# Three VectorE intermediates moved from SBUF to PSUM, and a later turn for the variance sum

## The chip, the cores and the metric

One Trainium2 chip, one core of it. The metric is the device time of one execution in microseconds. TensorE (PE in the rows) multiplies matrices from SBUF into PSUM; VectorE (DVE), ScalarE (ACT) and GpSimd (POOL) do elementwise work; SyncE (SP) issues the transfers. All operands of GpSimd in this kernel are in SBUF.

## The reference

Two layers over 512 latent tokens of width 2048, all in float32. Each weight is split into a rounded part and a rest (`whi`, `wlo`), so that every product is three matmuls.

```
# even layer, path A (chunked spatial gating), one of 8 channel groups g
v     = rms_norm(gelu(h @ Wav)) split into 4 chunks of 128 positions
mixed = einsum('qp,npc->nqc', w_s[g], v[:, :, g]) + b_s[g]
ya    = gelu(h @ Wau) * mixed * silu(h @ Wag)
# path B: differential attention; then x1 = x + gt * (concat(ya, yb) @ Wout)

# odd layer (Conformer convolution module)
y = a * sigmoid(b)                        # a, b, g = split(h @ w_in, 3)
y = depthwise_conv31(y) + dw_b
y = silu(layer_norm(y, ln_g, ln_b))       # mean and variance over 2048 channels
x = x1 + gt * ((y * silu(g)) @ w_out)
```

## The kernel before

Activations stand with channels on the 128 partitions and the 512 tokens along the row, so a tile is 128x512 float32 and there are 16 of them per tensor (`KT` = 16). Weights come in granules of 1 MB: SP loads `raw` (3 buffers), ScalarE rounds it to `whi` (line 100), VectorE or GpSimd takes the difference `wlo` (line 101), 2 buffers each. A granule of the odd layer feeds 48 matmuls of 512 columns (4 output tiles x 4 input tiles x 3 products).

A scheduler of the language sets the order of every engine's instructions from the order of the code and from its own guess of durations; the order is fixed when the kernel is built. Three places matter here.

1. **Mixing**, lines 637 to 656. Twice (`ug`), four groups: ScalarE makes `gu` = gelu (3 buffers), TensorE makes the mixing product `z` in a PSUM slot, VectorE computes `mx = z*gvh + bsb` (line 651) and `mx = mx*gu` (line 655), and SP stores `mx` (2 buffers) to `ug_s`. The PSUM pool `psM` has two slots of one bank; `zt()` and later `z4()` take them in turn, and the first tiles of the attention stage (`fm`, line 726) take the same two. When attention begins, SP's queue holds behind the last store of `mx` the loads of `kk` and `qq` (lines 763 and 766), whose memory overlaps what mixing used.
2. **Layer norm**, `ln_chain`, lines 1067 to 1088. It is a generator: each granule of the last gate groups (`g_group`, lines 1090 to 1092) takes one step of it through its hook. `mb` is the mean, spread by a matmul; VectorE subtracts it from the 16 tiles `zs` (line 1071), ScalarE squares (`sq`, 2 buffers), VectorE adds the squares into `vacc` (line 1077). TensorE then sums `vacc` over the partitions (line 920, in `token_rstd`), GpSimd takes the power, TensorE spreads the result (line 201), VectorE multiplies (line 1082), ScalarE applies gain and bias (1083) and tanh (`th`, 1085, 2 buffers of the same tag as `sq`), and VectorE finishes the swish (line 1086).
3. **The products for the output**, lines 1095 to 1100: `zs*sg` (line 1097), its rounding `y2h` (line 108) and rest `y2l` (line 109), read by the last 256x3 matmuls. In the same stretch GpSimd makes the `wlo` of each granule.

Of the kernel before, what the change touches and what calls it, by code (L numbers as in the profile page):

```python
# [13 lines left out]
AF = mybir.ActivationFunctionType  # L14
ALU = mybir.AluOpType
# [4 lines left out]
P = 128  # L20
D = 2048
KT = D // P
T = 512
NT = T // P
# [21 lines left out]
def hybrid_layers_kernel(  # L46
# [7 lines left out]
    V, A, G, PE, SP = nc.vector, nc.scalar, nc.gpsimd, nc.tensor, nc.sync  # L54
# [7 lines left out]
    def nm(s):  # L62
        uid[0] += 1
        return f"{s}_{uid[0]}"

    def mm(o, l, r, start, stop):
        return PE.matmul(o, l, r, start=start, stop=stop)  # L67
# [44 lines left out]
    def t_group(W, c0, mov, pool, tag, ntile=4, nk=4, lo_eng=None, hook=None, prologue=None):  # L112
        ncols = ntile * P
        ps = [pool.tile([P, T], F32, tag=tag, name=nm("tg")) for _ in range(ntile)]
        for gi in range(KT // nk):
            hi, lo = load_w(W, gi * nk * P, nk, c0, ncols, lo_eng)
            for j in range(ntile):
                for k in range(nk):
                    kt = gi * nk + k
                    mh, ml = mov[kt]  # L120
                    wh, wl = hi[:, k, j * P : (j + 1) * P], lo[:, k, j * P : (j + 1) * P]
                    mm(ps[j], wh, mh, kt == 0, False)
                    mm(ps[j], wl, mh, False, False)
                    mm(ps[j], wh, ml, False, kt == KT - 1)
            if hook:
                hook(gi)
        return ps
# [60 lines left out]
    def rstd_cols(dst, src, scale, tmp):  # L188
        n = dst.shape[1]
        V.tensor_scalar(tmp, src, scale, EPS, op0=ALU.mult, op1=ALU.add)  # L190
        G.tensor_tensor(dst, tmp, mhalf[:, 0:1].broadcast_to([P, n]), op=ALU.pow)  # L191

    def spread_cols(dst_ps, col, diag):
        n = col.shape[1]
        V.tensor_tensor(
            diag.rearrange("p (t q) -> p t q", q=P),
            ident.unsqueeze(1).broadcast_to([P, n, P]),
            col.unsqueeze(2).broadcast_to([P, n, P]),
            op=ALU.mult,
        )  # L200
        PE.matmul(dst_ps, ones, diag, start=True, stop=True)
# [9 lines left out]
    gvh = cp.tile([P, 8], F32, name="gvh")  # L211
# [15 lines left out]
    def zt(n=T):  # L227
        return psM.tile([P, n], F32, tag="m", name=nm("z"))
# [24 lines left out]
    th = tp.tile([P, 2 * KT], F32, tag="small", name="th")  # L253
# [347 lines left out]
    bsb = c2.tile([P, 8, P], F32, name="bsb")  # L601
# [35 lines left out]
    for ug in range(2):  # L637
        ps = t_group(e_w_in, C_U + 512 * ug, hm, psA, "m", hook=hook2)
        for j in range(4):
            g = 4 * ug + j  # L640
            gu = bp.tile([P, T], F32, tag="gu", bufs=3, name=nm("gu"))
            A.activation(gu, ps[j], AF.Gelu)
            z = zt()
            for n in range(NT):
                o_ = z[:, n * P : (n + 1) * P]
                vh, vl = vn[n][0][:, g * P : (g + 1) * P], vn[n][1][:, g * P : (g + 1) * P]
                mm(o_, vh, wsh[:, g, :], True, False)
                mm(o_, vh, wsl[:, g, :], False, False)
                mm(o_, vl, wsh[:, g, :], False, True)
            mx = bp.tile([P, T], F32, tag="mx", name=nm("mx"))  # L650
            V.scalar_tensor_tensor(
                mx.rearrange("p (n q) -> p n q", q=P), z.rearrange("p (n q) -> p n q", q=P), gvh[:, g : g + 1],
                bsb[:, g, :].unsqueeze(1).broadcast_to([P, NT, P]), op0=ALU.mult, op1=ALU.add,
            )
            V.tensor_tensor(mx, mx, gu, op=ALU.mult)
            SP.dma_start(ug_s[g], mx)
    p12.close()

# [248 lines left out]
    def z4(n=T):  # L907
        return psM.tile([P, n], F32, tag="m", name=nm("z4"))
# [4 lines left out]
    def tt(s, tag, bufs=1, n=T):  # L913
        return t4.tile([P, n], F32, tag=tag, bufs=bufs, name=nm(s))

    def token_rstd(acc, t0, t1, scale):
        n = (t1 - t0) // P
        z = z4(n)
        for t in range(n):
            PE.matmul(z[:, t : t + 1], acc[:, t0 + t * P : t0 + (t + 1) * P], ones[:, 0:1], start=True, stop=True)  # L920
        r = tt("r", "r", 2, n)
        rstd_cols(r, z, scale, r)
        dg = tt("dg", "b", 1, t1 - t0)
        z = z4(t1 - t0)
        spread_cols(z, r, dg)
        return z
# [83 lines left out]
    zs = [None] * KT  # L1010
# [54 lines left out]
    vacc = tt("vacc", "qacc")  # L1065

    def ln_chain():
        mb = z4()
        PE.matmul(mb, onesn, macc, start=True, stop=True)
        for i in range(KT):  # L1070
            V.tensor_tensor(zs[i], zs[i], mb, op=ALU.subtract)
            if i == 0:
                A.activation(vacc, zs[i], AF.Square)
            else:
                sq = tt("sq", "a", 2)
                A.activation(sq, zs[i], AF.Square)
                V.tensor_tensor(vacc, vacc, sq, op=ALU.add)  # L1077
            if i % 4 == 3:
                yield
        rb3 = token_rstd(vacc, 0, T, 1.0 / D)  # L1080
        for i in range(KT):
            V.tensor_tensor(zs[i], zs[i], rb3, op=ALU.mult)
            A.activation(zs[i], zs[i], AF.Identity, bias=g2[:, cLB + i : cLB + i + 1], scale=g2[:, cLG + i : cLG + i + 1])
            th = tt("th", "a", 2)
            A.activation(th, zs[i], AF.Tanh, scale=0.5)
            V.scalar_tensor_tensor(zs[i], th, 1.0, zs[i], op0=ALU.add, op1=ALU.mult)
            if i % 4 == 3:
                yield

    chain = ln_chain()  # L1090
    for gi in range(1, 4):
        g_group(gi, lambda gi: next(chain, None))
# [10 lines left out]
    for og in range(4):  # L1103
        ps = t_group(o_w_out, 512 * og, y2m, psA, "m", lo_eng=G)
        for j in range(4):
            i = 4 * og + j
# [3 lines left out]
            z = z4()  # L1110
# [47 lines left out]
```

## Time and profile before

| what | value |
|---|---|
| median of 3 runs | 1890.2 us (1884.23 to 1893.12) |
| the profiled execution's own time | 1880.81 us |
| its span (first to last instruction) | 1879.0 us |
| TensorE busy | 1818.0 us, 97% |
| VectorE / ScalarE / GpSimd busy | 1124.1 / 581.8 / 484.6 us (60 / 31 / 26%) |
| mean granted TensorE clock | 0.993 of full |

The span is cut into instructions; an engine's idle time is put down to whatever released it. The profiled execution lies 9.4 us below the median, just under the lowest of the three runs. Times in rows are microseconds from the start of the span.

### The profile page before, as it was taken

What the parts mean: (1) busy time and instruction counts of PE and PEld (TensorE: products, weight loads), DVE (VectorE), ACT (ScalarE), POOL (GpSimd) and SP (SyncE); (2) the same over time, 40 slices, a digit from 0 to 9 for tenths busy, and PEclk for the clock granted to TensorE, in tenths of its full rate; (3) what the DMA queues carried; (4) which work ended last, traced back from release to release, by engine and by line L of the source; (5) the groups of instructions that cost most, each with busy time, mean ns of one, the idle gap of its engine ahead of it and who ended that gap; (6) DMA issues with size and microseconds to landing.
All of it is one profiled execution on the core that took longest, in us unless ns stands there. A gap on an engine that the chain in (4) does not pass through costs nothing.

```text
span 1879.0 us, 21854 instructions
## 1 busy us (share of the span) xinstructions
PE 1818.0 (97%) x8744; PEld 1480.8 (79%) x8744; DVE 1124.1 (60%) x1527; ACT 581.8 (31%) x769; POOL 484.6 (26%) x191
## 2 busy tenths in 40 slices
PE   5999999999999999999999999999999999999998
PEld 2558888888788788888878779888888888778886
DVE  4348436367666536667664346169999999693000
ACT  3322212222331234444433335222222222473221
POOL 0002002011000122323212213345445445444431
PEclk9999999999999999999999999999999999999999
DMA  9996745648978577557645652322332332224441
GB/s 319 339 332 210 224 139 180 201 155 283 314 255 296 190 191 198 150 149 194 215 166 202 216 194 84 107 95 90 102 100 90 98 104 90 90 74 136 138 134 57
DMA packets 220390, 324.16 MB, mean 173 GB/s; under 512 B 10169, under 2 KB 139522, under 8 KB 212098
## 3 DMA queue, kind: packets, MB, share of 16 engines
q1 hardware_dynamic: 220290, 322.77, 53.9%
q8 instruction: 69, 1.13, 0.2%
q14 instruction: 31, 0.25, 0.0%
HBM read 289.18 MB, written 33.55 MB: 172 GB/s over the span
## 4 chain that ended last, share of the span: by engine, by line
PE 78%; DMA 9%; DVE 5%; issue 4%; POOL 1%; ACT 1%; SPq 1%; DVEq 0%; POOLq 0%; ACTq 0%
PE tg L67 37%; PE mb L67 17%; PE fm L67 9%; PE m L67 7%; DMA raw<-in_o_ada_w_dram 5%; PE S L67 2%; DMA raw<-in_e_ada_w_dram 2%; PE oT L67 2%; PE z L301 1%; DVE acc L460 1%; DVE wlo L101 1%; POOL wlo L101 1%; DVE vacc L1077 1%; PE t L815 1%; DMA x<-in_x_dram 1%
## 5 line engine op out<-in xcount | busy, mean ns | idle before, releaser
L101 POOL TENSOR_TENSOR wlo<-raw,whi 128x2048 fp32r<-128x2048 f32 x84 | 396.7, 4723 | 719.4 <-ACT whi L100 711.4
L100 ACT CAST whi<-raw 128x2048 fp32r<-128x2048 f32 x136 | 259.7, 1909 | 629.5 <-PE tg L67 272.6
L1041 DVE SCALAR_TENSOR_TENSOR z<-y,dwc,z 128x512 f32<-128x512 f32 x480 | 319.1, 740 | 0.1
L67 PE MATMUL tg<-h2h,wlo 128*128 128x512 f32 x704 | 275.4, 391 | 0.0
L67 PE MATMUL tg<-h2l,whi 128*128 128x512 f32 x704 | 274.6, 390 | 0.0
L67 PE MATMUL tg<-h2h,whi 128*128 128x512 f32 x704 | 271.0, 390 | 0.0
L460 DVE SCALAR_TENSOR_TENSOR acc<-raw,silu_c,acc 128x2048 f32<-128x2048 f32 x60 | 143.7, 2394 | 130.6 <-DMA raw<-in_o_ada_w_dram 82.7
L67 PE MATMUL mb<-whi,hhi 128*128 128x512 f32 x512 | 202.2, 397 | 2.6 <-ACT avt L622 2.0
L101 DVE TENSOR_TENSOR wlo<-raw,whi 128x2048 fp32r<-128x2048 f32 x52 | 119.1, 2290 | 140.1 <-ACT whi L100 140.1
L67 PE MATMUL mb<-wlo,hhi 128*128 128x512 f32 x512 | 201.2, 393 | 0.6 <-DVE wlo L101 0.6
L67 PE MATMUL mb<-whi,hlo 128*128 128x512 f32 x512 | 201.1, 393 | 0.0
L67 PEld LDWEIGHTS tg<-h2l,whi 128*128 128x128 f32 x704 | 132.6, 188 | 28.2 <-issue 0.5
L67 PEld LDWEIGHTS tg<-h2h,wlo 128*128 128x128 f32 x704 | 132.4, 188 | 27.9 <-issue 0.5
L67 PEld LDWEIGHTS tg<-h2h,whi 128*128 128x128 f32 x704 | 132.6, 188 | 27.5
L191 POOL TENSOR_TENSOR rs<-ms,mhalf 128x8 f32<-128x8 f32 x20 | 37.0, 1864 | 376.6 <-DVE ms L190 376.6
L67 PEld LDWEIGHTS mb<-whi,hhi 128*128 128x128 f32 x512 | 96.7, 189 | 36.0 <-issue 13.6
L67 PEld LDWEIGHTS mb<-wlo,hhi 128*128 128x128 f32 x512 | 96.7, 189 | 20.4 <-DVE wlo L101 1.0
L67 PEld LDWEIGHTS mb<-whi,hlo 128*128 128x128 f32 x512 | 96.7, 189 | 20.1
L67 PE MATMUL fm<-hhi,whi 128*128 128x512 f32 x256 | 106.8, 417 | 0.0
L1109 DVE SCALAR_TENSOR_TENSOR xr<-tg,gt,xr 128x512 f32<-128x512 f32 x16 | 11.9, 750 | 157.2 <-PE tg L67 125.2
L67 PE MATMUL tg<-y2h,wlo 128*128 128x512 f32 x256 | 99.9, 390 | 3.1 <-POOL wlo L101 3.1
L67 PE MATMUL fm<-hlo,whi 128*128 128x512 f32 x256 | 101.4, 396 | 0.0
(251 smaller groups left out, 3125.6 us busy)
## 6 DMA issues: line engine op xcount, KB each, us to landing
raw<-in_e_w_in_dram SPq DMA_DIRECT2D x56, 1024.0 KB, 5.3
raw<-in_o_ada_w_dram SPq DMA_DIRECT2D x48, 1024.0 KB, 6.5
raw<-in_o_w_in_dram SPq DMA_DIRECT2D x48, 1024.0 KB, 5.1
raw<-in_e_ada_w_dram SPq DMA_DIRECT2D x64, 512.0 KB, 8.2
raw<-in_e_ada_w_dram SPq DMA_DIRECT2D x16, 1024.0 KB, 5.1
raw<-in_e_w_out_dram SPq DMA_DIRECT2D x16, 1024.0 KB, 5.5
raw<-in_o_w_out_dram SPq DMA_DIRECT2D x16, 1024.0 KB, 5.1
qq<-q_s SPq DMA_DIRECT2D x16, 512.0 KB, 7.1
```

The lines of the kernel that those rows point to most:

```text
L67: return PE.matmul(o, l, r, start=start, stop=stop)
L100: A.copy(hi, raw)
L101: (lo_eng or V).tensor_tensor(lo, raw, hi.bitcast(F32), op=ALU.subtract)
L191: G.tensor_tensor(dst, tmp, mhalf[:, 0:1].broadcast_to([P, n]), op=ALU.pow)
L301: PE.matmul(ada_ps[j][32 * g : 32 * g + 32, 0 : 2 * nc_], S[:, kt, :], raw[:, i, :], start=(kt < 4), stop=(kt >= KT - 4), skip_group_check ...
L460: V.scalar_tensor_tensor(ada_state["acc"], raw, sc_[:, jt : jt + 1], ada_state["acc"], op0=ALU.mult, op1=ALU.add)
L815: PE.transpose(z[:, k * P : (k + 1) * P], e[:, (k0 + k) * P : (k0 + k + 1) * P], ident)
L1041: V.scalar_tensor_tensor(zi if t == TAPS - 1 else z, y2[:, t : t + T], w(t), z, op0=ALU.mult, op1=ALU.add)
L1077: V.tensor_tensor(vacc, vacc, sq, op=ALU.add)
L1109: V.scalar_tensor_tensor(xr, ps[j], gt2[:, i : i + 1], xr, op0=ALU.mult, op1=ALU.add)
```

## The change

Four edits. In mixing, line 651 writes its result back into the PSUM tile `z` instead of the SBUF tile `mx`, and line 655 reads `z` and `gu`; `mx` is written once. In layer norm, the running sum of squares lives in a PSUM tile `vp` taken from the pool `psM`; only the last addition writes `vacc` in SBUF, which the matmul of line 920 reads. A further `yield` stands between the last addition and `token_rstd`. And `th` is a PSUM tile from `psM` instead of an SBUF tile.

```
             z3 = z.rearrange("p (n q) -> p n q", q=P)
+            V.scalar_tensor_tensor(
+                z3, z3, gvh[:, g : g + 1], bsb[:, g, :].unsqueeze(1).broadcast_to([P, NT, P]), op0=ALU.mult, op1=ALU.add,
+            )
             mx = bp.tile([P, T], F32, tag="mx", name=nm("mx"))
-            V.scalar_tensor_tensor(
-                mx.rearrange("p (n q) -> p n q", q=P), z.rearrange("p (n q) -> p n q", q=P), gvh[:, g : g + 1],
-                bsb[:, g, :].unsqueeze(1).broadcast_to([P, NT, P]), op0=ALU.mult, op1=ALU.add,
-            )
-            V.tensor_tensor(mx, mx, gu, op=ALU.mult)
+            V.tensor_tensor(mx, z, gu, op=ALU.mult)
...
+        vp = z4()
         for i in range(KT):
             V.tensor_tensor(zs[i], zs[i], mb, op=ALU.subtract)
             if i == 0:
-                A.activation(vacc, zs[i], AF.Square)
+                A.activation(vp, zs[i], AF.Square)
             else:
                 sq = tt("sq", "a", 2)
                 A.activation(sq, zs[i], AF.Square)
-                V.tensor_tensor(vacc, vacc, sq, op=ALU.add)
+                V.tensor_tensor(vacc if i == KT - 1 else vp, vp, sq, op=ALU.add)
             if i % 4 == 3:
                 yield
+        yield
         rb3 = token_rstd(vacc, 0, T, 1.0 / D)
...
-            th = tt("th", "a", 2)
+            th = z4()
```

The built order of instructions shows what becomes of it. First VectorE in the first round of mixing (`z` and `mx` carry running numbers; `wlo` is the difference of a weight granule, `acc` a running product for the modulation vectors).

```order
-L651 SCALAR_TENSOR_TENSOR mx_4226<-z_4213,gvh,bsb 128x512
+L651 SCALAR_TENSOR_TENSOR z_4213<-z_4213,gvh,bsb 128x512
 L460 SCALAR_TENSOR_TENSOR acc_3836<-raw_4389,silu_c,acc_3836 128x2048
-L655 TENSOR_TENSOR mx_4207<-mx_4207,gu_4192 128x512
-L655 TENSOR_TENSOR mx_4226<-mx_4226,gu_4211 128x512
-L651 SCALAR_TENSOR_TENSOR mx_4245<-z_4232,gvh,bsb 128x512
-L651 SCALAR_TENSOR_TENSOR mx_4264<-z_4251,gvh,bsb 128x512
-L655 TENSOR_TENSOR mx_4245<-mx_4245,gu_4230 128x512
-L655 TENSOR_TENSOR mx_4264<-mx_4264,gu_4249 128x512
+L655 TENSOR_TENSOR mx_4208<-z_4194,gu_4192 128x512
+L655 TENSOR_TENSOR mx_4227<-z_4213,gu_4211 128x512
+L651 SCALAR_TENSOR_TENSOR z_4232<-z_4232,gvh,bsb 128x512
```

`z` is now read until line 655, so its slot comes free later; TensorE's products for `z_4232` and `z_4251` were moved behind 26 more matmuls of the weights. In the second round (`z_4527` to `z_4584`) the order is the same as before: 651 and 655 in turn.

Second, TensorE around the variance sum, line 920, before and then of the change (`tg` is an output tile of the gate product, `h2h` and `h2l` its inputs).

```order
L67 MATMUL tg_11916<-h2h_8675,wlo_12154 128x512
L67 MATMUL tg_11916<-h2l_8676,whi_12153 128x512
L920 MATMUL z_1776_11971<-ones,vacc_11616 128x1 x4
L67 MATMUL tg_11916<-h2h_8681,whi_12153 128x512
L67 MATMUL tg_11916<-h2h_8681,wlo_12154 128x512
```

```order
L67 MATMUL tg_11917<-h2h_8675,wlo_12135 128x512
L67 MATMUL tg_11917<-h2l_8676,whi_12134 128x512
L920 MATMUL z_1780_12026<-ones,vacc_11616 128x1 x4
L67 MATMUL tg_11917<-h2h_8681,whi_12134 128x512
L67 MATMUL tg_11917<-h2h_8681,wlo_12135 128x512
```

Only the numbers differ: the variance sum stands three matmuls before the end of the same granule, and the spreading matmul of line 201 stands 24 matmuls behind that granule in both. The further `yield` changes the numbering and not this place.

Third, ScalarE at the start of the tanh of layer norm, before and then of the change.

```order
L1083 ACTIVATE z_9906<-z_9906,g_86 128x512
L1083 ACTIVATE z_9940<-z_9940,g_86 128x512
L1085 ACTIVATE th_11985<-z_9906 128x512
L1083 ACTIVATE z_9974<-z_9974,g_86 128x512
L1085 ACTIVATE th_11990<-z_9940 128x512
L1083 ACTIVATE z_10008<-z_10008,g_86 128x512
```

```order
L1085 ACTIVATE z_9906<-z_9906,g_86 128x512
L1085 ACTIVATE z_9940<-z_9940,g_86 128x512
L1087 ACTIVATE z_1784_12040<-z_9906 128x512
L1085 ACTIVATE z_9974<-z_9974,g_86 128x512
L1085 ACTIVATE z_10008<-z_10008,g_86 128x512
L1085 ACTIVATE z_10510<-z_10510,g_86 128x512
```

The second tanh (`z_1785`) now stands behind 15 of the 16 gain-and-bias steps, because its PSUM slot holds the spread factor until VectorE's last multiplication; the first keeps its place. Smaller moves: the `wlo` of the first granule of the odd layer stands two additions earlier on VectorE, and TensorE's last matmuls of that part alternate between two output tiles; two loads of `xr` for the end stand some twenty loads earlier on SP.

## Rows read from the trace of the kernel before

**Rows 1.** The page, busy time by engine (busy us, share of span, instructions).

```profile
PE 1818.0 (97%) x8744; PEld 1480.8 (79%) x8744; DVE 1124.1 (60%) x1527; ACT 581.8 (31%) x769; POOL 484.6 (26%) x191
```

**Rows 2.** Waits of TensorE: who waited for whom, total us, times, longest us.

```profile
PE z L67 <- DVE mx L651: 3.8, 1, 3.8
...
PE z L920 <- DVE vacc L1077: 2.8, 1, 2.8
```

**Rows 3.** Timeline of VectorE, second mixing round: start us, us, instruction, idle before.

```profile
646.48 0.75 DVE L651 SCALAR_TENSOR_TENSOR mx<-z,gvh,bsb 128x512 f32<-128x512 f32 x1 [8.08 <-PE z L67]
647.33 4.90 DVE L655 TENSOR_TENSOR mx<-mx,gu 128x512 f32<-128x512 f32 x1
652.16 0.74 DVE L651 SCALAR_TENSOR_TENSOR mx<-z,gvh,bsb 128x512 f32<-128x512 f32 x1
...
654.74 0.75 DVE L651 SCALAR_TENSOR_TENSOR mx<-z,gvh,bsb 128x512 f32<-128x512 f32 x1 [1.04 <-DMA ug_s<-mx]
```

**Rows 4.** Timeline of GpSimd, the same stretch.

```profile
647.17 4.52 POOL L101 TENSOR_TENSOR wlo<-raw,whi 128x2048 fp32r<-128x2048 f32 x1 [1.54 <-ACT whi L100]
```

**Rows 5.** Timeline of TensorE: fourth mixing product, first attention fill.

```profile
652.95 0.45 PE L67 MATMUL z<-wsh,vnh 128*128 128x128 f32 x1 [3.83 <-DVE mx L651]
...
655.64 0.77 PE L67 MATMUL fm<-hhi,whi 128*128 128x512 f32 x1
```

**Rows 6.** Windows: us, busy us by engine (instructions), PEclk (share of full), DMA share, GB/s.

```profile
652.90:659.60 6.70, 6.65 (x21) 5.75 (x22) 3.49 (x5) 0.00 (x0) 0.00 (x0) 0.51 0.56 170
...
1638.30:1644.00 5.70, 5.70 (x22) 4.73 (x23) 2.48 (x5) 2.38 (x2) 2.03 (x2) 0.70 0.31 121
```

**Rows 7.** Timeline of SP's transfers from 645; last row: size, median us to landing.

```profile
645.66 0.37 SPq L92 DMA_DIRECT2D raw<-in_e_w_in_dram  x1
...
652.26 4.37 SPq L656 DMA_DIRECT2D ug_s<-mx  x3
656.73 0.38 SPq L92 DMA_DIRECT2D raw<-in_e_w_in_dram  x1
657.77 0.32 SPq L656 DMA_DIRECT2D ug_s<-mx  x1
663.06 1.33 SPq L763 DMA_DIRECT2D kk<-k_s  x2
...
raw<-in_e_w_in_dram SPq DMA_DIRECT2D x2, 1024.0 KB, 5.3
```

**Rows 8.** Timeline of VectorE in layer norm.

```profile
1606.84 9.65 DVE L1071 TENSOR_TENSOR z<-z,z 128x512 f32<-128x512 f32 x16 [8.36 <-PE z L1069]
1616.41 13.66 DVE L1077 TENSOR_TENSOR vacc<-vacc,sq 128x512 f32<-128x512 f32 x12
1631.51 5.47 DVE L1077 TENSOR_TENSOR vacc<-vacc,sq 128x512 f32<-128x512 f32 x2 [1.44 <-ACT sq L1076]
...
1637.49 0.68 DVE L1077 TENSOR_TENSOR vacc<-vacc,sq 128x512 f32<-128x512 f32 x1
```

**Rows 9.** Timeline of GpSimd in layer norm.

```profile
1604.61 4.61 POOL L101 TENSOR_TENSOR wlo<-raw,whi 128x2048 fp32r<-128x2048 f32 x1 [3.20 <-ACT whi L100]
1616.40 5.16 POOL L101 TENSOR_TENSOR wlo<-raw,whi 128x2048 fp32r<-128x2048 f32 x1 [7.18 <-ACT whi L100]
```

**Rows 10.** Lines 1071, 1077, 1041: durations min/median/max ns, first and last start.

```profile
L1071 DVE TENSOR_TENSOR z<-z,z x16: 677/679/689, 1606.8 to 1615.8; 128x512 f32<-128x512 f32 x16
...
L1077 DVE TENSOR_TENSOR vacc<-vacc,sq x15: 681/692/4908, 1616.4 to 1637.5; 128x512 f32<-128x512 f32 x15
...
L1041 DVE SCALAR_TENSOR_TENSOR z<-y,dwc,z x480: 728/740/756, 1240.8 to 1597.7; 128x512 f32<-128x512 f32 x160
```

**Rows 11.** Timelines of GpSimd, VectorE and TensorE where the output product begins.

```profile
1679.37 9.10 POOL L101 TENSOR_TENSOR wlo<-raw,whi 128x2048 fp32r<-128x2048 f32 x1 [7.92 <-ACT whi L100]
...
1684.57 4.45 DVE L1097 TENSOR_TENSOR z<-z,sg 128x512 f32<-128x512 f32 x1
...
1688.52 0.50 PE L67 MATMUL tg<-y2h,wlo 128*128 128x512 f32 x1 [2.15 <-POOL wlo L101]
...
1701.34 0.50 PE L67 MATMUL tg<-y2h,wlo 128*128 128x512 f32 x1 [0.95 <-POOL wlo L101]
```

More of the change, by code (lines that the diff above doesn't have):

```diff
@@ L649, in hybrid_layers_kernel @@
                 mm(o_, vl, wsh[:, g, :], False, True)
+            z3 = z.rearrange("p (n q) -> p n q", q=P)
+            V.scalar_tensor_tensor(
+                z3, z3, gvh[:, g : g + 1], bsb[:, g, :].unsqueeze(1).broadcast_to([P, NT, P]), op0=ALU.mult, op1=ALU.add,
+            )
             mx = bp.tile([P, T], F32, tag="mx", name=nm("mx"))
-            V.scalar_tensor_tensor(
-                mx.rearrange("p (n q) -> p n q", q=P), z.rearrange("p (n q) -> p n q", q=P), gvh[:, g : g + 1],
-                bsb[:, g, :].unsqueeze(1).broadcast_to([P, NT, P]), op0=ALU.mult, op1=ALU.add,
-            )
-            V.tensor_tensor(mx, mx, gu, op=ALU.mult)
+            V.tensor_tensor(mx, z, gu, op=ALU.mult)
             SP.dma_start(ug_s[g], mx)
```

## The prediction

> **What bounds the kernel.** I read the page first: TensorE is busy 97% of the span [rows 1], so only what shortens TensorE's idle time, or its stretches at half clock, can shorten the kernel. The list of TensorE's waits comes next, because it says which idle time the change can touch. Two of its entries end at instructions that the diff edits: 3.8 us in mixing and 2.8 us at the variance sum [rows 2]. Then I went to the timelines of those places. In mixing, line 655 multiplies two SBUF tiles and takes 4.90 us, not the 0.69 us of its neighbours; it begins just after GpSimd's `wlo` and ends just after it [rows 3, 4]. In layer norm the additions of line 1077 read two SBUF tiles and reach 4908 ns where the median is 692, while the subtractions of line 1071, which read one SBUF tile and one PSUM tile, stay at 677 to 689 ns although GpSimd worked beside them from 1604.61 to 1609.2 [rows 8, 9, 10]. So the reader should see one mechanism: a VectorE instruction with two SBUF inputs stands still while GpSimd's tensor operation runs, and one with a single SBUF input does not. Last, the windows: after both waits TensorE runs at half clock for a while, 0.51 granted over 6.7 us after the first, and 0.70 over 5.7 us after the second [rows 6]. A wait costs more than its length.
>
> **Mixing, second round.** What it loses now: until 655.64, when the first attention fill starts, and then at half clock until 659.6. Those 4.0 us at half clock are worth 2.0 us, so the stage ends as if it had gone on at full clock from 657.6 [rows 5, 6].
> After the change the first 651 still runs at 646.48 and 655 at 647.33, now 0.69 us long: done at 648.0 rather than 652.2. The PSUM slot is now held until 655 ends, not until 651 ends at 647.2, so the third product starts about 0.5 us late. The twelve matmuls of a product took 2.7 us at half clock [rows 5], so 1.35 at full: third product until 649.4, and the fourth, whose slot is free at 649.5 after the second 655, until 650.9. What is late next is the third 655: it writes an `mx` buffer whose store must have landed. That store is issued at 648.05, behind a 1 MB weight load issued at 645.66, which takes 5.3 us and lands at 651.0 [rows 7]. A store with nothing ahead let VectorE go on 2.5 us after its issue (652.26 to 654.74) [rows 3, 7]; behind the load I bound its end from 651.0 (rides along) to 653.5 (starts when the load has landed), and take 652.2, as the store's own 256 KB are a quarter of the load. The third 655 then runs to 652.9 and the first fill, which takes that slot, starts at 653.0 at full clock. Gain: 657.6 - 653.0 = 4.6 us, with the bounds 3.3 and 5.8.
> One limit behind it: the loads of `kk` wait for the last store, which stands behind another 1 MB load (5.3 us from 657.77 to 663.06) [rows 7]. They move with the third 655: that load issues at 653.0 instead of 656.73, so `kk` starts about 3.4 us earlier, at 659.7. The first scores come 72 matmuls after the first fill, so the loads' lead shrinks by about 1.2 us; I count nothing for it and leave it to the range, whose mixing term I cut to 5 us at the top.
>
> **Mixing, first round.** GpSimd is idle there, nothing was blocked, nothing is gained. The slot is held until 655, but the scheduler placed the third and fourth product behind 26 more matmuls (some 6 us), which covers the roughly 3 us that it takes longer. Cost nothing; without that cover it would be those 3 us.
>
> **Layer norm.** Two of the fifteen additions stood behind GpSimd: the first twelve took 13.66 us where eleven steps of 0.8 and one of 0.7 make 9.5, so 4.1 too long; the next two 5.47 for 1.5, so 4.0 too long [rows 8]. As `vp` is in PSUM, both fall away: the last addition ends near 1638.2 - 8.1 = 1630.1. TensorE reached line 920 2.8 us before 1638.2, at 1635.4 [rows 2, 8], and its place in the order has not moved. The wait goes with 5 us to spare. Price: 2.8 us, and the half clock behind it. At a granted 0.70 over 5.7 us, 3.4 us were at half, worth 1.7. With 0.2 us for starting up again, 4.7 us.
> The trace has no addition that writes PSUM. Below it lies 0.68 us (line 1071, PSUM read), above it 0.74 (line 1041, PSUM read and written) [rows 10]; at 0.74 the fifteen cost 0.9 us more, inside the 5 us. One square and sixteen tanh of ScalarE now write PSUM too. For these I take no change, as VectorE's rows show none; the square, the first of the chain, could cost its whole length again and stay inside the 5 us, and tanh runs ahead of a VectorE that is the slower there.
> [...]
> The `yield` costs nothing: TensorE's order is unchanged. `th` in PSUM: line 1086 is no longer blocked, but what follows it on VectorE, lines 1097 and 109, still reads two SBUF tiles and takes the block instead (4.45 us on line 1097 already now [rows 11]). Gain on the chain: near nothing. TensorE waits there only for `wlo`, 2.15 and 0.95 us [rows 11], since GpSimd stands still in turn while VectorE's two-input instructions follow one another (9.10 us instead of 4.6). With single-input instructions among them GpSimd gets in sooner, but TensorE also arrives sooner by the gap that goes; I take 0, with bounds -2 and +3.4.
>
> **Elsewhere.** Around 1170 the `wlo` that moved up on VectorE holds the last additions of the norm before it by 2 us; alternating matmuls cover most of it. I take -0.4 us, bounds -1.5 and +0.5.
>
> **Sum.** 4.6 + 4.7 + 0 - 0.4 = 8.9 us. The profiled execution's own time, 1880.8, becomes 1871.9. It lies 9.4 us under the median, so against the median: 1890.2 - 8.9 = 1881.3 us, -0.47%.
>
> **Rivals.**
> *A, the output product's waits go too.* For it: GpSimd's 9.10 us is caused by VectorE's two-input instructions, of which 16 go. Against: TensorE comes earlier. Then 4.6 + 4.7 + 3.1, with its two restarts, some 12.5 us: 1877.7.
> *B, the mixing gain is taken by a new wait.* The slot is held longer and the third 655 hangs on a store; if the 0.5 and 2 us that TensorE waits then bring the half clock back for as long as now (6.7 us, worth 3.4), mixing gives 1.2 us and the whole 5.5: 1884.7. For: 2.8 us idle brought it. Against: 2.15 us did not, at 1688 [rows 11].
> *C, slower: the output product becomes paced by GpSimd.* All four granules of the first output group wait for a whole `wlo` (4.6 us) and each wait brings the half clock (1.7 us): 25 us lost, 16 net, 1906. It decides from the point at which each of the four waits passes 2.2 us (8.9 in all). For: two of the four wait already, and tanh now waits for a PSUM slot. Against: fewer instructions compete with GpSimd.
>
> **Chances.** Forecast (7 to 10.5 us) 0.47; A (10.5 to 14) 0.23; B (3 to 7) 0.21; C and less than 3 us 0.09. What this kernel's measurement can tell from no change is about 0.5%, 9.5 us. Faster by more: all of A and a third of the forecast, 0.39. Slower by more: most of C, 0.05. Within: 0.56. The range, from 1875 (A at its far end, with 1 us) to 1888 (B's far end, 3 us gained, and 1 us), leaves out C and the tails of A and B. The forecast alone: 1879.7 to 1883.2.
>
> **What would show it.** Right: line 655 at 0.7 us throughout, no wait of TensorE at line 920 and none of 3.8 us in mixing, no half clock after 1638, additions of line 1078 all near 0.7 us. Wrong: a wait of the first `fm` or third `z` beyond 2.5 us; half clock at 655; waits for `wlo` near 1690 above 2.2 us each; scores waiting for `kk` or `qq`.

## The result, and the profile after

| kernel, timing | median us (runs) | kernel before beside it | ratio, 95% interval |
|---|---|---|---|
| the change, first | 1877.55 (6) | 1890.93 | 0.994 (0.9921 to 0.996) |
| the change, second | 1877.01 (6) | 1887.06 | 0.9937 (0.9913 to 0.9961) |
| the change, third | 1877.14 (11) | 1887.22 | 0.9949 (0.9931 to 0.9968) |

The change is faster by 0.5 to 0.6%, 10 to 13 us between the medians. The forecast was 1881.3, in a range of 1875 to 1888; the measured time lies in the range, and below the 1879.7 to 1883.2 of the forecast alone. The profiled execution has a span of 1876.6, only 2.4 us below that of before; why that is less than the medians say comes at the end of this section and with the first experiment.

The page of the changed kernel, busy time by engine, answers to [rows 1]. TensorE's total is the same within 0.4 us: no work has gone.

```profile
PE 1818.4 (97%) x8744; PEld 1481.2 (79%) x8744; DVE 1110.6 (59%) x1527; ACT 581.6 (31%) x769; POOL 479.6 (26%) x191
```

TensorE's waits of the changed kernel that answer to [rows 2] and [rows 11] (who waited for whom, total us, times, longest):

```profile
PE tg L67 <- POOL wlo L101: 1.9, 1, 1.9
...
PE S L67 <- ACT th L736: 1.6, 1, 1.6
PE fm L67 <- DVE mx L655: 1.4, 1, 1.4
...
PE z L67 <- DVE mx L655: 0.4, 1, 0.4
```

The 3.8 us at the fourth product (the start that [rows 5] show) and the 2.8 us at line 920 are gone. In place of the first stand 0.4 us at the third product and 1.4 at the first attention fill, and the wait at the first scores (`S`) has grown from 0.5 to 1.6.

**Mixing, second round.** VectorE, GpSimd and TensorE there, and the window behind the first fill; they answer to [rows 3 to 6].

```profile
649.16 0.76 DVE L651 SCALAR_TENSOR_TENSOR z<-z,gvh,bsb 128x512 f32<-128x512 f32 x1 [8.35 <-PE z L67]
650.01 0.69 DVE L655 TENSOR_TENSOR mx<-z,gu 128x512 f32<-128x512 f32 x1
...
651.46 0.69 DVE L655 TENSOR_TENSOR mx<-z,gu 128x512 f32<-128x512 f32 x1
...
654.41 0.69 DVE L655 TENSOR_TENSOR mx<-z,gu 128x512 f32<-128x512 f32 x1 [1.24 <-DMA ug_s<-mx]
```

```profile
649.85 4.55 POOL L101 TENSOR_TENSOR wlo<-raw,whi 128x2048 fp32r<-128x2048 f32 x1 [1.37 <-ACT whi L100]
```

```profile
655.25 0.47 PE L67 MATMUL fm<-hhi,whi 128*128 128x512 f32 x1 [1.43 <-DVE mx L655]
```

```profile
655.20:661.90 6.70, 6.65 (x29) 5.54 (x30) 1.26 (x2) 0.00 (x0) 0.00 (x0) 1.00 0.76 238
```

GpSimd's operation runs from 649.85 to 654.40, and line 655 passes it twice in 0.69 us. The third 655 waits for the store, the first fill starts 6.1 us after the first 651 (655.25 - 649.16), and the clock stays at full. Before it took 9.2 us, and then 4.0 us at half clock, worth 2.0.

The gain reaches the scores only as far as their loads come forward. TensorE's first score before, then of the change SP's last store, the first `kk` load behind it, and the first score:

```profile
674.73 0.59 PE L67 MATMUL S<-kk,qq 128*128 128x256 f32 x2 [0.51 <-issue]
```

```profile
656.58 0.32 SPq L656 DMA_DIRECT2D ug_s<-mx  x1
661.87 1.33 SPq L763 DMA_DIRECT2D kk<-k_s  x2
...
673.42 1.65 PE L67 MATMUL S<-kk,qq 128*128 128x256 f32 x8 [1.56 <-ACT th L736]
```

Counted from the first 651, the first `kk` load is issued at 16.6 us before and at 12.7 in the change, 3.9 earlier; the first score comes 11.7 us after it before and 11.6 in the change, and 11.4 to 11.7 in all six profiles with the whole mixing edit (18.9 to 19.1 after the start of the third 655). The row of the wait names ScalarE's `th`, but that had ended 0.9 us before the score, and in the run with the product in PSUM (below) it ends 0.7 us after it. So the loads, and not `th`, are what the scores hang on.

**Layer norm.** The fifteen additions, line 1078 (1077 before), and GpSimd beside them; they answer to [rows 8 to 10].

```profile
1618.37 9.54 DVE L1078 TENSOR_TENSOR z<-z,sq 128x512 f32<-128x512 f32 x12
1629.72 1.50 DVE L1078 TENSOR_TENSOR z<-z,sq 128x512 f32<-128x512 f32 x2 [1.81 <-ACT sq L1077]
...
1631.73 0.68 DVE L1078 TENSOR_TENSOR vacc<-z,sq 128x512 f32<-128x512 f32 x1
```

```profile
1618.37 4.63 POOL L101 TENSOR_TENSOR wlo<-raw,whi 128x2048 fp32r<-128x2048 f32 x1 [7.18 <-ACT whi L100]
1629.24 4.62 POOL L101 TENSOR_TENSOR wlo<-raw,whi 128x2048 fp32r<-128x2048 f32 x1 [6.24 <-ACT whi L100]
```

Twelve take 9.54 us instead of 13.66, two take 1.50 instead of 5.47, with GpSimd at work beside both. The last ends at 1632.4, and TensorE comes to line 920 at 1637.2, 4.8 us later.

**Where a loss came in**, at the norm ahead of the odd layer: TensorE's spreading matmul of line 201 and ScalarE's copy of it, first of the kernel before and then of the changed one.

```profile
1162.66 0.60 PE L201 MATMUL z<-dg,ones 128*128 128x256 f32 x2
...
1163.30 0.37 ACT L965 COPY rbs<-z 128x256 f32<-128x256 f32 x1 [1.37 <-PE z L201]
```

```profile
1164.21 0.60 PE L201 MATMUL z<-dg,ones 128*128 128x256 f32 x2
...
1164.85 0.37 ACT L965 COPY rbs<-z 128x256 f32<-128x256 f32 x1 [2.97 <-PE z L201]
...
1177.92 0.50 PE L67 MATMUL m<-h2h,wlo 128*128 128x512 f32 x1 [1.22 <-DVE wlo L101]
```

The diff does not touch these lines. The order of TensorE does change here: the spreading matmul stands 19 places later, the multiplications behind it start 1.55 us later, and TensorE ends by waiting 1.22 us for VectorE's `wlo`. How much that costs hangs on the granted clock ahead of the spreading matmul. The whole stretch (the fifth column of the table below) in the first and the second profile of the change:

```profile
1145.67:1203.97 58.30, 54.20 (x330) 48.71 (x330) 32.83 (x58) 27.51 (x46) 19.01 (x26) 0.97 0.30 95
```

```profile
1142.70:1199.99 57.29, 53.19 (x330) 47.45 (x330) 32.83 (x58) 27.51 (x46) 19.01 (x26) 1.00 0.30 97
```

At full clock the new order costs 1.0 us; with a stretch at half clock in it (0.97) 2.0, and at 0.94, in the run with the product in PSUM, 3.1. In the old order the stretch is 56.3 us at 0.97 as well as at 1.00, and 56.9 at 0.94.

**Account by stretch.** Each kernel that ran left a profile. The table has for each the time from the start of one instruction to the start of another: where the first line 651 of the second round starts (ahead of every place where I expect a gain or loss); from there to the first score; from there to GpSimd's first multiplication of the norm ahead of the odd layer (line 972); from there to GpSimd's second `wlo` after it; from the first subtraction of the layer norm to the spreading of its variance; from there to the end of the span. Before: 646.48, 674.73, 1145.72, 1202.01, 1606.84, 1647.23.

| profile | first 651 at | mixing to scores | scores to 972 | norm ahead of odd layer | variance sum | to the end |
|---|---|---|---|---|---|---|
| before | 646.48 | 28.25 | 470.99 | 56.29 | 40.39 | 231.77 |
| before, against itself | 647.56 | 28.01 | 478.59 | 56.26 | 40.37 | 232.29 |
| the change, first | 649.16 | 24.26 | 472.25 | 58.30 | 35.71 | 232.09 |
| the change, second | 647.44 | 23.43 | 471.83 | 57.29 | 35.71 | 231.77 |
| the change, third | 644.89 | 23.97 | 472.15 | 58.30 | 35.71 | 232.16 |
| only mixing | 645.81 | 23.56 | 472.86 | 58.31 | 41.65 | 231.68 |
| only variance sum | 647.78 | 28.18 | 470.45 | 56.30 | 35.71 | 232.55 |
| only tanh | 648.00 | 28.12 | 470.65 | 56.29 | 40.38 | 231.63 |
| without tanh | 647.20 | 24.24 | 472.02 | 58.33 | 35.71 | 232.58 |
| two groups | 651.72 | 25.14 | 470.77 | 56.29 | 35.71 | 231.84 |
| two groups, three mx | 651.54 | 23.89 | 481.11 | 56.88 | 35.71 | 231.85 |
| rest on VectorE | 650.89 | 28.45 | 470.00 | 56.28 | 40.34 | 232.22 |
| squares in PSUM | 644.95 | 28.06 | 472.28 | 56.28 | 35.71 | 232.60 |
| product in PSUM | 652.02 | 24.05 | 470.19 | 59.42 | 35.70 | 228.19 |

The change, as the mean of its three profiles against the first of before: -4.4 in mixing to the scores (28.25 - 23.89), +1.7 at the norm, -4.7 at the variance sum, +0.2 to the end, together -7.2 us. Two stretches are left out. From GpSimd's second `wlo` to the first subtraction it is 404.8 us in all fourteen. From the scores to line 972 the change has 1.1 us more on average; apart from the two profiles with 478.6 and 481.1, of which the first experiment speaks, that stretch goes from 470.0 to 472.9 in kernels with and without the edit, so I count it to neither. A difference of two spans says little: the first line 651 alone starts anywhere from 644.9 to 652.0, with most of that spread ahead of any edit, as the two rows of the kernel before and the three of the change show. From the first 651 to the end, the three profiles of the change are 5.1 to 7.7 us shorter than the first profile of before, and 12.9 to 15.5 shorter than the second.

### The profile page after: what moved, and what is told of

Read it like the earlier page. It is cut to its first block, busy times and chain, and to the rows that moved or that the text cites. A ratio compares the mean times of both kernels' runs of the same rounds, so it can differ in the third digit from the quotient of the medians.

```text
span 1876.6 us, 21858 instructions
## 1 busy us (share of the span) xinstructions
PE 1818.4 (97%) x8744; PEld 1481.2 (79%) x8744; DVE 1110.6 (59%) x1527; ACT 581.6 (31%) x769; POOL 479.6 (26%) x191
## 4 chain that ended last, share of the span: by engine, by line
PE 79%; DMA 8%; DVE 5%; issue 4%; POOL 1%; ACT 1%; SPq 1%; DVEq 0%; POOLq 0%; ACTq 0%
PE tg L67 39%; PE mb L67 17%; PE fm L67 9%; PE m L67 6%; DMA raw<-in_o_ada_w_dram 5%; PE S L67 2%; DVE acc L460 2%; PE z L301 2%; PE oT L67 2%; DVE wlo L101 1%; DMA raw<-in_e_ada_w_dram 1%; PE t L815 1%; POOL wlo L101 1%; DMA x<-in_x_dram 1%; DMA q_s<-qklo 0%
## 5 line engine op out<-in xcount | busy, mean ns | idle before, releaser
L101 POOL TENSOR_TENSOR wlo<-raw,whi 128x2048 fp32r<-128x2048 f32 x84 | 390.3, 4646 | 714.8 <-ACT whi L100 706.8
```

What stands on the lines that cost most here:

```text
L101: (lo_eng or V).tensor_tensor(lo, raw, hi.bitcast(F32), op=ALU.subtract)
```

## The experiments

The theories: **S**, the edits work each at its own place, with the sizes of the table; **R**, the medians moved more than these places show because the timed runs of the kernel before contain something that its first profile lacks. Other rivals are named where they are tried. In edits a line with - is of the kernel named ahead of it.

### The kernel before against itself

> The unchanged kernel against itself, to see how large a difference is without any edit and to get a second profile of it. Ratio 1.000, with an interval of about 0.3% to either side. Theory S (the gain comes from the two places alone, some 5 us in the two profiled executions once a clock drop near 515 us is left out): the second profile looks like the first, with TensorE waiting 3.8 us in mixing and 2.8 us at the variance sum, and a span within 3 us of 1879. Rival R (the timed runs of the kernel before contain something that its first profiled execution, 9.4 us below the median, did not): this profile has a span of 1885 us or more, and stretches at half clock or waits that the first one lacks.

Measured: ratio 1.0016 (1.0001 to 1.0031), 1889.25 against 1886.52. So 0.2% is what the same kernel can differ from itself, and the interval, which leaves out 1, is too narrow. The profile has a span of 1887.9, 9 us over the first one, as R said. VectorE, GpSimd and TensorE at the place that differs most, in the first profile of before, then in this one, and the window behind it:

```profile
1096.26 2.29 DVE L101 TENSOR_TENSOR wlo<-raw,whi 128x2048 fp32r<-128x2048 f32 x1
...
1096.71 6.30 POOL L101 TENSOR_TENSOR wlo<-raw,whi 128x2048 fp32r<-128x2048 f32 x1 [19.50 <-ACT whi L100]
...
1098.60 0.50 PE L67 MATMUL m<-yh,wlo 128*128 128x512 f32 x1 [2.84 <-DVE wlo L101]
```

```profile
1098.23 6.58 DVE L101 TENSOR_TENSOR wlo<-raw,whi 128x2048 fp32r<-128x2048 f32 x1
...
1098.16 4.50 POOL L101 TENSOR_TENSOR wlo<-raw,whi 128x2048 fp32r<-128x2048 f32 x1 [19.49 <-ACT whi L100]
...
1104.87 0.79 PE L67 MATMUL m<-yh,wlo 128*128 128x512 f32 x1 [7.65 <-DVE wlo L101]
```

```profile
1098.00:1110.00 12.00, 5.13 (x13) 4.08 (x14) 9.51 (x6) 2.32 (x5) 4.50 (x1) 0.57 0.60 182
```

It is the mechanism of the change at a place where the change does nothing. Two operations with two SBUF inputs each, one of VectorE and one of GpSimd, become ready together; the one that starts first takes its normal time (VectorE 2.29 us, GpSimd 4.50) and the other stands (GpSimd 6.30 us, VectorE 6.58). VectorE was 0.45 us ahead in the first profile; here GpSimd was ahead by 0.07, TensorE waited 4.8 us longer and went on at half clock, a granted 0.57 over the 12 us of the last row, and the stretch from the scores to line 972 is 7.6 us longer (table). Of the fourteen profiles GpSimd was first in two.

### The parts

Each has one part of the diff alone: the hunk of lines 650 to 655; the hunks with `vp` and `yield`; the hunk with `th`.

> Only the mixing edit. Theory S: the first attention fill starts about 6 us after the first line 651 at full clock, where it took 9.2 us and then 4 us at half clock before: -5.0 us there. Around 1160 to 1180 TensorE's order is that of the whole change (the spreading matmul 19 places later), which costs 2.6 us; the scores wait 1 us longer. Net about -1.5 us, ratio 0.999. Rival R: as the medians moved by 13 us with the whole change, this edit alone gives 6 us or more, ratio 0.997 or less.

Measured: ratio 0.9979 (0.9963 to 0.9995). The gain to the scores (23.56 us) and the loss at the norm (58.31) both belong to this edit; the wait at line 920 stays. S holds in the profile in kind (net -2.7 us for the two, where S had -1.5); the ratio lies between the two theories and its interval holds both. The stretch of the variance sum is 1.3 us longer here than before (41.65 against 40.39), behind the same wait of 2.8 us: the granted clock over the 6.7 us after it is 0.54, where before it was 0.75.

> Only the variance sum in PSUM and its later turn. No other instruction of TensorE moves. Theory S: no wait at line 920, no half clock behind it, -4.7 us, ratio 0.9975; the waits for the weight rests at the output product stay about 3 us together. Rival A: with TensorE earlier by 4.7 us the waits at the output product grow by as much, ratio 1.000. Rival R: 8 us or more, ratio 0.996 or less.

Measured: ratio 0.9975 (0.9962 to 0.9988), as S said: 35.71 us in its stretch, 56.30 at the norm. Rival A's giving back is small, 0.8 us to the end: TensorE waits 2.1 us for GpSimd at the output product, and the granted clock is 0.83 over the 10 us from 1680, where before it stayed at full.

> Only tanh in PSUM. Theory S: ratio 1.000; line 1086 stays at 0.7 us beside GpSimd where it reached 4.8, but lines 1097 and 109 take the block, and the wait at line 920 is unchanged at 2.8 us; the waits for the weight rests at the output product stay between 1 and 5 us together. Rival A: GpSimd gets in sooner, the two waits for it (2.15 and 0.95 us) go, -3 us, ratio 0.998. Rival C: tanh waiting for its PSUM slot holds up VectorE and TensorE waits 5 us or more there, ratio 1.003.

Measured: ratio 1.0015 (1.0001 to 1.003), which is what the kernel before has against itself. Two groups by line and GpSimd's timeline at the start of the output product:

```profile
L1086 DVE SCALAR_TENSOR_TENSOR z<-z,z x16: 674/678/691, 1658.9 to 1701.3; 128x512 f32<-128x512 f32 x16
...
L1097 DVE TENSOR_TENSOR z<-z,sg x16: 675/679/4614, 1659.6 to 1704.3; 128x512 f32<-128x512 f32 x16
```

```profile
1680.52 4.94 POOL L101 TENSOR_TENSOR wlo<-raw,whi 128x2048 fp32r<-128x2048 f32 x1 [7.89 <-ACT whi L100]
```

Line 1086 is never held any more, line 1097 takes the block, and GpSimd's operation shrinks from 9.10 us [rows 11] to 4.94. TensorE still waits 2.6 us there in two parts, and the stretch to the end is the same. S; the variance sum is as late as before in this kernel.

The further `yield` had no run of its own: with it alone the built order of the instructions is that of before on all five engines.

### The whole once more, and without tanh

> The whole change once more, beside its parts. Theory S (the edits add up, each at its own place): from the profiles of the parts -2.7 us for mixing (-5.65 at the place, +1.0 at the scores, +2.0 around 1170), -4.7 for the variance sum, 0 for tanh, together -7.4 us, ratio 0.996. Rival D: the edits give more together than apart, ratio 0.994 as in the first timing.

Measured: ratio 0.9937 (0.9913 to 0.9961), and 0.9949 (0.9931 to 0.9968) in a third timing.

> The whole change a third time, for comparison within this call: ratio 0.994 to 0.996.

> The whole change without the tanh edit. Theory S: tanh gives nothing, so this is as good as the whole change, ratio 0.994 to 0.996, and the waits for GpSimd at the output product are 2 to 3 us in both. Rival D (the whole is more than its parts because tanh helps once the variance sum is early): 2 us or more slower than the whole change in the same call.

Measured for the change without tanh: ratio 0.9963 (0.9946 to 0.9979), a median of 1878.58 against 1877.14 for the whole beside it. The parts give 0.9979 x 0.9975 = 0.9954 without tanh, and 0.9969 with tanh's 1.0015; the whole gives 0.9937 to 0.9949, each with some 0.2% to either side and a kernel that differs from itself by as much. S and D can't be told apart by these times. The profiles speak for D in kind and against its size: where the variance sum is early, the stretch to the end is 232.6 us in the three profiles with tanh in SBUF and 231.8 to 232.2 in the five with tanh in PSUM (the product still in SBUF), some 0.6 us less.

### The blocker is GpSimd, and two SBUF inputs

Of the kernel before:

```
-            return load_w(jobs[n][2], gi * 8 * P, 8, jobs[n][3], 2 * P, G)
+            return load_w(jobs[n][2], gi * 8 * P, 8, jobs[n][3], 2 * P, V if n == 0 else G)
```

> The kernel before, but the rests (wlo) of the first two weight granules of the attention stage are computed by VectorE, so that GpSimd stands idle beside the second round of mixing; line 655 still reads two SBUF tiles. Theory S (GpSimd's tensor operation is what holds line 655): all eight of line 655 at 0.7 us, TensorE's 3.8 us wait at the third product gone or under 1 us, no half clock behind it; less the 2.3 us each that VectorE now spends on the two rests, -3 to -5 us, ratio 0.998. Rival G (line 655 is slow for another reason, its SBUF output or the store that runs beside it): the first 655 of the second round stays near 4.9 us, ratio 1.000.

Measured: ratio 1.0013 (0.9993 to 1.0033). Line 655 by its durations (min/median/max ns), and VectorE's timeline:

```profile
L655 DVE TENSOR_TENSOR mx<-mx,gu x8: 680/682/692, 609.8 to 662.4; 128x512 f32<-128x512 f32 x8
```

```profile
650.89 0.75 DVE L651 SCALAR_TENSOR_TENSOR mx<-z,gvh,bsb 128x512 f32<-128x512 f32 x1 [2.97 <-PE z L67]
651.56 2.28 DVE L101 TENSOR_TENSOR wlo<-raw,whi 128x2048 fp32r<-128x2048 f32 x1
...
660.49 1.42 DVE L651 SCALAR_TENSOR_TENSOR mx<-z,gvh,bsb 128x512 f32<-128x512 f32 x2 [4.66 <-DMA ug_s<-mx]
```

G falls: two SBUF inputs with no GpSimd beside them run in 0.68 us. The gain that I expected did not come. VectorE's own 2.28 us stands between lines 651 and 655, a weight load slips ahead of the first store, and the third 651 waits 4.66 us for that store. TensorE waits 1.6 + 3.4 us where it waited 3.8.

Again of the kernel before:

```
-                sq = tt("sq", "a", 2)
+                sq = z4()
```

> The kernel before with one edit: the squares (sq) are PSUM tiles, while the running sum vacc stays in SBUF, read and written there. Theory S (VectorE is held only if both inputs are in SBUF): additions of 0.7 us beside GpSimd, no wait at line 920, ratio 0.9975 as with the sum in PSUM. Rival W (what counts is that the running sum is not written to SBUF): additions of 4.9 us as before, a wait of 2.8 us at line 920, ratio 1.000.

Measured: ratio 0.9972 (0.9954 to 0.999). Line 1077 of this kernel, and GpSimd beside it:

```profile
L1077 DVE TENSOR_TENSOR vacc<-vacc,z x15: 676/689/690, 1616.0 to 1629.3; 128x512 f32<-128x512 f32 x15
```

```profile
1615.96 4.63 POOL L101 TENSOR_TENSOR wlo<-raw,whi 128x2048 fp32r<-128x2048 f32 x1 [7.18 <-ACT whi L100]
```

The sum is read from and written to SBUF as before, only the second input is in PSUM, and no addition is held: the longest takes 690 ns, where the held ones of before reached 4.9. W falls: here the second SBUF input is what counts. Line 655 shows the same beside GpSimd, 4.90 us with two SBUF inputs and 0.69 with one, and at 1098 a head start of 0.07 us decided who stands, 6.58 against 2.29 us for VectorE.

### Taking the loss back

Of the changed kernel; the second of the two runs has the last line as well (and so has the other tile of that tag, `junk`). Lines below stand one further in these kernels: 652 and 656.

```
+            mx = bp.tile([P, T], F32, tag="mx", name=nm("mx"))
+            m1 = z if ug and j < 2 else mx
             V.scalar_tensor_tensor(
-                z3, z3, gvh[:, g : g + 1], bsb[:, g, :].unsqueeze(1).broadcast_to([P, NT, P]), op0=ALU.mult, op1=ALU.add,
+                m1.rearrange("p (n q) -> p n q", q=P), z.rearrange("p (n q) -> p n q", q=P), gvh[:, g : g + 1],
+                bsb[:, g, :].unsqueeze(1).broadcast_to([P, NT, P]), op0=ALU.mult, op1=ALU.add,
             )
-            V.tensor_tensor(mx, z, gu, op=ALU.mult)
+            V.tensor_tensor(mx, m1, gu, op=ALU.mult)
...
+            mx = bp.tile([P, T], F32, tag="mx", bufs=3, name=nm("mx"))
```

> The whole change, but in mixing only the first two groups of the second round keep their result in PSUM, the six others go through mx as before. TensorE's spreading matmul then stands one place later around 1160, not nineteen. Theory S (the one thing that mixing gains is the first line 655 of the second round, and what it loses around 1170 is the later spreading matmul): first attention fill as early as with the whole edit, no second wait there, 2.0 to 2.6 us better than the whole change, ratio 0.995. Rival E: the loss around 1170 is not from that order, ratio as the whole change.

> As the run with two groups, and mx has three buffers, so that the third group does not wait for the landing of the first store. Theory S: the wait of the first attention fill (1.4 us) goes, and 1.0 to 1.4 us are gained on top of the run with two groups, ratio 0.9945. Rival F: the scores wait for their loads behind the same 1 MB weight loads as before, so that what is gained at the fill is lost at the scores, ratio as the run with two groups.

Measured: ratios 0.9958 (0.9939 to 0.9977) and 0.9968 (0.9948 to 0.9988). With two groups the stretch of the norm is 56.29 us again, so the loss comes from the order there, as S said. VectorE's `wlo` is back in its old place too; that the spreading matmul is what counts is read from the rows above, where the multiplications are late ahead of any `wlo`. But the mixing stretch is 25.14 us, where the whole edit has 23.4 to 24.3, because the third line 652 writes `mx` again and waits 2.53 us for the store. S had the fill as early as with the whole edit; it comes 6.4 us after the first 652. TensorE at the first fill, and the window behind it:

```profile
658.14 0.47 PE L67 MATMUL fm<-hhi,whi 128*128 128x512 f32 x1 [1.75 <-DVE mx L652]
```

```profile
658.10:664.10 6.00, 5.96 (x19) 4.82 (x20) 2.04 (x3) 0.00 (x0) 0.00 (x0) 0.72 0.67 203
```

The wait is 1.75 us, and half clock is back. With three buffers the first fill waits for nothing and comes 4.5 us after the first line 652, and then the scores stand, with the clock down behind them:

```profile
675.43 2.85 PE L67 MATMUL S<-kk,qq 128*128 128x256 f32 x8 [2.85 <-issue]
```

```profile
672.00:684.00 12.00, 9.15 (x36) 7.30 (x35) 3.22 (x6) 3.75 (x6) 1.79 (x1) 0.86 1.09 232
```

Rival F: what is won at the fill is lost at the scores. This profile is also the second in which GpSimd was first at 1099 (8.7 us of wait there), and both kernels are no better than the change.

### One operation more

Of the changed kernel:

```
+        yp = z4()
-        V.tensor_tensor(zs[i], zs[i], sgs[i], op=ALU.mult)
+        V.tensor_tensor(yp, zs[i], sgs[i], op=ALU.mult)
         hi, lo = htile("y2h"), htile("y2l")
-        split(hi, lo, zs[i])
+        split(hi, lo, yp)
```

> The whole change, and the product of line 1099 goes into a PSUM tile, from which ScalarE rounds it and VectorE takes the rest: 16 more VectorE instructions read one SBUF input, the 16 of line 1099 still read two. Rival A of the prediction (the waits for GpSimd at the output product can go as well): GpSimd gets in between, its first wlo there takes under 6.5 us where it took 9.1, the waits of TensorE for it (1.9 to 2.7 us) go, 2 to 4 us better than the whole change, ratio 0.992. Theory S: the block moves to the 16 that are left and the two PSUM slots hold VectorE up instead; the waits stay or grow, ratio 0.994 to 0.997.

Measured: ratio 0.9931 (0.9911 to 0.9952), a median of 1873.65 (6 runs) where the change beside it had 1877.14. The same window of TensorE in the kernel before, the change and this one:

```profile
1676.00:1716.00 40.00, 36.90 (x162) 29.90 (x161) 28.93 (x36) 19.45 (x26) 22.25 (x4) 1.00 0.28 92
```

```profile
1676.00:1716.00 40.00, 38.12 (x161) 31.07 (x160) 26.49 (x32) 17.45 (x24) 18.70 (x4) 0.96 0.24 79
```

```profile
1676.00:1716.00 40.00, 40.00 (x178) 33.13 (x177) 29.98 (x34) 16.68 (x24) 18.88 (x4) 1.00 0.24 81
```

No wait and no half clock is left in it, and the stretch to the end is 228.2 us where it was 231.8 and 232.1. The waits that rival A named are gone, worth 3.9 us against the change, from an edit that this change doesn't have. Its mechanism is not shown: GpSimd's operation there, in the change and then in this kernel, is no shorter.

```profile
1692.48 4.56 POOL L101 TENSOR_TENSOR wlo<-raw,whi 128x2048 fp32r<-128x2048 f32 x1 [10.79 <-ACT whi L100]
```

```profile
1688.83 5.05 POOL L101 TENSOR_TENSOR wlo<-raw,whi 128x2048 fp32r<-128x2048 f32 x1 [7.88 <-ACT whi L100]
```

It starts 5.3 us earlier, counted from the spreading of the variance (42.6 us behind it, 48.0 in the change), and so does ScalarE's cast ahead of it (40.6 and 46.0). Why the cast comes earlier, by the other order of ScalarE's work or by the PSUM tile itself, no run separates. This is the fastest kernel of the study by its median.

The same profile has a first attention fill that waits less than that of the change, and the clock falls behind it:

```profile
657.90 0.47 PE L67 MATMUL fm<-hhi,whi 128*128 128x512 f32 x1 [1.22 <-DVE mx L655]
```

```profile
657.90:664.60 6.70, 6.70 (x22) 5.36 (x23) 1.21 (x2) 0.00 (x0) 0.00 (x0) 0.75 0.76 238
```

It cost nothing at the scores: they come 24.05 us after the first 651, as in the change, and TensorE no longer waits there. What it lost at half clock it would have waited for the loads.

## Why the prediction was right, and where it was not

**Variance sum: right in mechanism and size.** -4.7 us forecast; 40.39 - 35.71 = 4.68 in all nine profiles in which the additions have one SBUF input. Both terms (the wait, and the half clock behind it) fell away. The second term is not a fixed size: with only the mixing edit the same wait cost 1.3 us more. The 0.2 us for starting up again was my estimate and no run shows it by itself; the first matmul after the wait at 1688.52 of before takes 0.50 us, the ones behind it 0.39 to 0.40.

**Mixing: right up to the first fill, too high at the scores.** The third product was to start 0.5 us late: it waits 0.38 us and starts 1.68 us after the first 651, where it started 1.14 after it before. The third 655 was to hang on the store, and the first fill to start 6.5 us after the first 651 at full clock (6.1 in the first profile, 5.3 and 5.7 in the others of the change). From the first 651 to the fill the gain is 5.1 us, 4.6 forecast. The store's landing, taken at 5.7 us after the first 651 with bounds of 4.5 and 7.0, let the third 655 start at 5.3, 4.5 and 4.9: in the lower half. What I left to the range was the scores, and their loads are what bounds the stage: they came forward by 3.9 us and TensorE by 5.1, so TensorE waits 1.56 us where it waited 0.51, and 1.0 us is given back: net 4.0 in this profile, 4.4 in the mean of three. That the scores would wait for `kk` or `qq` was one of my own signs of being wrong.

**First round and `yield`: nothing, as forecast; tanh: near nothing.** TensorE waits for nothing in the first round, before and in the three profiles of the change. Tanh gives some 0.6 us in the last stretch once the variance sum is early, against 0.8 that the early variance sum gives back there.

**Price of PSUM: none that counts**, as the row of line 1071 had said [rows 10]. Line 655 with a PSUM source has a median of 692 ns, where with two SBUF inputs and no GpSimd beside it it had 682; line 1078 with a PSUM source and a PSUM target has 700, where the SBUF form had 692. ScalarE's tanh, which had no row, became shorter: 596 ns into PSUM and 632 into SBUF.

**Elsewhere: the step that failed.** I took -0.4 us, at worst -1.5, from additions that `wlo` holds up, and wrote that "alternating matmuls cover most of it". The loss is 2.0 us in four of the six profiles with the whole mixing edit (1.0 and 3.1 in the others), and 0 to 0.6 without it. I had read VectorE's and TensorE's order there and priced the two changes that I saw, but not the spreading matmul of line 201 that stands 19 places later in the same piece. All multiplications of the second half wait for it. The new order costs 1.0 us at full clock; the rest is half clock ahead of the spreading matmul, which the old order hid all but 0.6 us of.

**Output product: right in sum, not in its parts.** 0 forecast, +0.2 measured. GpSimd did get in sooner (4.94 us instead of 9.10), and of two waits one of 1.9 us is left, which is rival A's mechanism begun. But the granted clock behind that wait fell to 0.70 for 5.7 us in the first and third profile of the change. In the second, behind the same 1.88 us, it stayed at full, and a second wait of 0.78 us stands there. What decides that is open.

**The total: partly luck.** Its mechanisms come to -7.2 us in the profiles where I had -8.9; the medians moved by 10 to 13, with intervals that reach down to 6 to 7.5. So 3 to 6 us of the measured gain belong to no term of my sum. The number came out near rival A's 1877.7, and nearer to "faster by over 0.5%" (0.39) than to "within" (0.56), but not for A's reason. What may lie between is shown in kind, not in size: an execution in which GpSimd is first at 1098 loses 7.6 us, and the base of my sum, an execution of 1880.8, was one in which it was not. Whether the change makes such executions rarer is open. In five of six profiles of kernels with the whole mixing edit VectorE's head start there was 0.5 us or more, and 1.2 in two of them; in the eight others it was 0.5 or more in four, and GpSimd was first in two. That is too few to tell, and no run tried to move it.

**Rivals.** B's half clock did not come about in the three profiles of the change, where waits of 0.68 to 1.43 us left the clock at full. It did in the run with the product in PSUM, with the same mixing code and a wait of 1.22 us, and there it did not take the mixing gain, because the scores wait for their loads. C did not come about either: no granule of the first output group waits over 2.2 us.

## What to carry to other kernels

Where VectorE and GpSimd both work on SBUF, look for VectorE rows whose longest is several times their median (here 4908 against 692 ns), and give such an instruction one PSUM input: it cost at most 10 ns of some 690 here, and the gain is the wait that hangs on it and the half clock behind it, as far as the next thing that TensorE waits for lets them through (here the loads for the scores). Look for the same pair wherever runs of one kernel differ among themselves, because at 1098 the order of two starts decided 7.6 us. When a scheduler sets the order, compare the whole of it on the engine that is the bound, and price every instruction that has moved and has others waiting for it, also 500 us from the edit.

## What the runs showed that I had not expected

A head start of 0.07 us for GpSimd turned a VectorE operation of 2.29 us into one of 6.58 and cost the execution 7.6 us. And in these runs the clock's answer to a wait is not set by its length, nor by the place: at the first fill 1.43 us (change) left it at full, 1.22 (product in PSUM) brought it to 0.75 over 6.7 us and 1.75 (two groups) to 0.72 over 6; at the output product the same 1.88 us of the same kernel brought it to 0.70 over 5.7 us in one execution and left it at full in another. So one profile is not enough to say that a wait of some length is safe.
